# Expert slots regrouped from 28 to 24 units of 32, w1 and w3 interleaved in each weight block, and a new order table

## The chip, the cores and the metric

One core of a Trainium2 chip runs the whole program. The metric is the device time of one execution in microseconds; runs of the same kernel differ by a few tenths of a per cent. The profile is of one further execution of the same program.

## What is computed

Two blocks follow each other on 256 tokens of width 1024. The first mixes tokens with gated linear attention and then runs a mixture of experts; the second has two attention layers, for which a context of 256 tokens goes through the same layer beside the tokens. The change is in the experts of the first block:

```python
N_EXPERTS = 16; N_EXPERT_GROUPS = 4; TOP_K = 2; D_EXPERT = D_MODEL // 2      # D_MODEL = 1024

def _moe(h, w_router, b_router, w1, w3, w2):            # h: 256 tokens
    scores = jax.nn.sigmoid((h @ w_router).astype(jnp.float32))
    sel = scores + b_router.astype(jnp.float32)
    ...                                                  # the best group of 4 experts, and 2 of its 4
    gates = jnp.sum(jax.nn.one_hot(idx, N_EXPERTS, dtype=jnp.float32) * wts[..., None], axis=1)
    out = jnp.zeros_like(h)
    for e in range(N_EXPERTS):
        he = jax.nn.silu(h @ w1[e]) * (h @ w3[e])        # [256, 512]
        out = out + gates[:, e:e + 1] * (he @ w2[e])
    return out
```

Only the tokens that picked an expert need its products: 512 token and expert pairs in all. With the given inputs expert 0 has 37 tokens, and the others, sorted, have 71, 57, 50, 43, 41, 37, 32, 26, 23, 21, 21, 15, 14, 12 and 12.

## The kernel before

**Slots and ranks.** The chip counts the tokens of each expert and sorts the experts by count: rank 0 is the fullest, rank 15 is always expert 0. `RANKS` (line 23) fixes how many slots each rank has: 128 for rank 0, 64 for ranks 1 to 8 and 15, 32 for ranks 9 to 14. `SLOT0` gives where they start; 896 slots in all, 28 units of 32. Rank 8's 64 slots are cut into two halves (8 and 80) that share their weights. An expert with more tokens than slots would run through `overflow`, a loop that starts only if a count says so.

**Gather.** `gather` collects the rows of 256 slots at a time by products with one-hot matrices (`oh`) into tiles named `xg` (the first 64 slots and the last 64 into a `t` tile). There are five such groups, `ga0` to `ga4`.

**Rounds.** `plan` (line 2106) lists seven rounds, `moe0` to `moe6`. A round of kind 64 takes two experts one after the other; each is a *step*: `ffn` multiplies 64 rows with w1 and with w3, side by side in the two column halves of the array, 8 times over (the 1024 inputs in 8 parts, `kt`); then 4 transposes, the activation, and `down`, which multiplies with w2 in 4 parts, the two halves of the output side by side. A step of kind 32 does the same for two experts at once in four column quarters. `round128` takes rank 0 with all 128 columns, w1 and w3 one after the other. That is 13 steps: eight of 64 rows, one of 128, four of 32. `merge_y` ends a round: it adds 128 slots back to their tokens by one-hot products (`ps<-y,t`). All of these are fp32; a fp32 product leaves two records in the trace.

**Weights.** An expert's weights come in six blocks of 1 MB: `w1_0`, `w3_0` (kt 0 to 3), `w1_1`, `w3_1` (kt 4 to 7), `w2_0`, `w2_1`. `loadr` (line 1994) issues a block's DMA on SyncE's queue with an address from the rank; in the trace these are the rows of line 2005. Blocks of expert 0 and all other weights are issued at line 326. At most five blocks (`WC = 5`) are held at a time; a block's buffer is free when the last product with it has run.

**What sets the order.** Every instruction is recorded first and emitted later (so nearly all rows have line 326, the helper's): `Sched.emit` simulates the engines with the costs of `_cost` and lets each take the recorded instruction that is first in program order, moved by the number of its section in the table `PRI`. The context stream of block 2 (sections beginning with X: split weights `cv`, its rows `hh` and `hl`, later `KgT`, `PT` and softmax tiles `t`) is spread by `merge` between the rounds of the experts by DMA and TensorE cost. On the chip every engine runs its list strictly in that order.

```python
    plan = [([[15], [7]], 64), ([[0]], 128), ([[1], [2]], 64), ([[3], [4]], 64), ([[5], [6]], 64),
            ([[8, 80], [9, 10]], 32), ([[11, 12], [13, 14]], 32)]
```

Of the kernel before, what the change touches and what calls it, by code (L numbers as in the profile page):

```python
# [14 lines left out]
OP = mybir.AluOpType  # L15
# [4 lines left out]
CAP = 64  # L20
NE = 16
# Slots in the first round. The experts but number 0 by their number of tokens, then number 0.
RANKS = [128] + 8 * [64] + 6 * [32] + [64]
# where the slots of a rank start (rank 8: of its halves)
SLOT0 = {15: 0, 7: 64, 0: 128, 1: 256, 2: 320, 3: 384, 4: 448, 5: 512, 6: 576,
         8: 640, 80: 704, 9: 672, 10: 736, 11: 768, 12: 832, 13: 800, 14: 864}
NSLOT = 896


# ---------------------------------------------------------------- host: layout only  # L30
# [63 lines left out]
def _chunks(i):  # L94
    """The weight stream: name -> [128, n] block, each contiguous per partition."""
    out = {}
    mods = [np.asarray(i["w_mod"])[0], np.concatenate(list(np.asarray(i["mod_w_2"])), 1)]
    for b in range(2):
        m = _kt(mods[b])
        for s in range(3):  # L100
            for kt in range(8):
                if b or s:
                    out[f"mod{b}_{s}_{kt}"] = m[:, kt, s * 2048:(s + 1) * 2048]
    # the first set in two parts: the same half of its two vectors in each
    m = _kt(mods[0])[:, :, :2048].reshape(128, 8, 2, 2, 512)
    for h in range(2):
        for k2 in range(4):
            out[f"modh{h}_{k2}"] = m[:, 2 * k2:2 * k2 + 2, :, h]

    def two(name, w):  # L110
        w = _kt(w)
        out[name + "_0"] = w[:, :4]
        out[name + "_1"] = w[:, 4:]

    g = np.asarray(i["gla_w_in"])[0]
    for n, a in (("gk", 512), ("gv0", 1024), ("gv1", 1536), ("gq", 0), ("gr0", 2048), ("gr1", 2560)):
        two(n, g[:, a:a + 512])
    o = np.asarray(i["gla_w_out"])[0]
    two("go0", o[:, :512])
    two("go1", o[:, 512:])  # L120
    w1, w3, w2 = (np.asarray(i[n])[0] for n in ("w_gate_e", "w_up_e", "w_down_e"))
    for e in range(NE):
        two(f"e{e}w1", w1[e])
        two(f"e{e}w3", w3[e])
        w = _kt(w2[e])
        out[f"e{e}w2_0"] = w[:, :2]
        out[f"e{e}w2_1"] = w[:, 2:]
    a = np.asarray(i["ab_w_in_2"])[0]
    two("acq", a[:, 0:512])
    two("agq", a[:, 544:1056])  # L130
    two("akv", np.concatenate([a[:, 512:544], a[:, 1056:1312]], 1))
    two("ag0", a[:, 1312:1824])
    two("ag1", a[:, 1824:2336])
    out["auq"] = _kt(np.asarray(i["mla_w_uq_2"])[0])
    kv = np.asarray(i["mla_w_ukv_2"])[0].reshape(256, 8, 128)
    out["aukv"] = _kt(np.concatenate([kv[:, :, :64].reshape(256, 512), kv[:, :, 64:].reshape(256, 512)], 1))
    o = np.asarray(i["ab_w_out_2"])[0]
    two("ao0", o[:, :512])
    two("ao1", o[:, 512:])
    c = np.asarray(i["cd_w_in_2"])[0]  # L140
    two("cq", c[:, 0:512])
    two("ckv", c[:, 512:768])
    for n, b in (("cgb", 768), ("cgc", 1280), ("cgh", 1792), ("cg0", 2304), ("cg1", 2816)):
        two(n, c[:, b:b + 512])
    o = np.asarray(i["cd_w_out_2"])[0]
    two("co0", o[:, :512])
    two("co1", o[:, 512:])
    return out


def host(i):
    """Lays the inputs out for the chip (copies only); returns the arrays and where the parts lie."""
    W = {}
    ch = _chunks(i)
    where, off, flat = {}, 0, []
    for n, a in ch.items():
        a = a.reshape(128, -1)
        where[n] = (off, a.shape[1])
        off += a.size
        flat.append(np.ascontiguousarray(a).reshape(-1))  # L160
    W["w"] = where
    arrays = {"w": np.concatenate(flat)}
    (W["cst"], arrays["cst"]), (W["gc"], arrays["gc"]), arrays["msk"] = _consts()
    wga = np.asarray(i["gla_w_gate_a"])[0].transpose(1, 0, 2).reshape(1024, 32)
    conv = np.asarray(i["conv_w_2"])[0]
# [12 lines left out]
    wgb = np.zeros((4, 2, 16, 2, 512), np.float32)  # L178
    for z in range(2):
        wgb[:, z, :, z, :] = gb[z][None]  # L180
    arrays["wgb"] = wgb.reshape(128, 1024)
    rows = [np.asarray(i[n]).reshape(-1) for n in (
        "gla_b_gate", "final_g", "b_router", "mla_q_gain_2", "mla_k_gain_2", "gqa_q_gain_2", "gqa_k_gain_2",
        "win_q_gain_2", "win_k_gain_2", "win_sink_2")]
    arrays["row"] = np.concatenate(rows)
    for n in ("x", "ctx", "ctx_2"):
        arrays[n] = np.ascontiguousarray(np.asarray(i[n])[0])
    return arrays, W


# ---------------------------------------------------------------- the order of the instructions
# [44 lines left out]
NB = 17  # L236
NA = 8
CTXSEQ = "CKgGqsk ba"
CDSEQ = "kqc+x gB a+G o"
GLASEQ = "N q r+M k+l1 K v+L+2 R+3 f"  # L240


class Op:
    __slots__ = ("eng", "fn", "acc", "cost", "lat", "preds", "npred", "succs", "tiles", "name", "later", "cols", "table", "grp", "tiled")


class Sched:
    """Records the program's instructions and emits them in an order found by list scheduling: every engine
    takes the first instruction of the program order whose operands are ready. Tiles of a tag are given
    their buffers in program order, so an order that fits the buffers serially always completes."""  # L250

    LAT = {"PE": 197.0, "ACT": 216.0, "DVE": 128.0, "POOL": 150.0, "SP": 950.0, "SD": 950.0, "GD": 9000.0}
    TICK = 10240.0 / 3
    GAP = (87.0, 33.0, 7.0, 33.0)
    ISSUE = {"SP": 1250.0, "SD": 1250.0, "GD": 1500.0}

    def __init__(self, nc):
        self.nc = nc
        self.main = []
        self.cur = self.main  # L260
# [90 lines left out]
    def _cost(self, eng, fn, out, a, k):  # L351
        n = self._free(out)
        if fn == "dma_start":
            return out.partition_size() * n * 4 / 360.0
        if eng == "PE":
            r32 = a[1].dtype == F32R
            if fn == "transpose":
                return 56.0 if r32 else 109.5
            cyc = 1 if r32 else 4
            m = out.partition_size()  # L360
            if m <= 64 and not r32:
                return (n * cyc / 2.4 + 77.0) / 4 if m <= 32 else (n * cyc / 2.4 + 22.0) / 2
            return max(n * cyc / 2.4, 107.0 if r32 else 210.0) + 2.5
# [20 lines left out]
    def together(self):  # L384
        """The instructions recorded inside (one engine's) are issued back to back."""
        return self._Together(self)
# [18 lines left out]
    class _Into:  # L405
# [8 lines left out]
        def __exit__(self, *a):  # L414
            self.s.cur = self.old

    def into(self, lst):
        return self._Into(self, lst)

    def merge(self, lst, i0, i1, other=1.0, later=0, dma=None):  # L420
        """Spreads the instructions of lst evenly (by tensor-engine time, and `other` for each instruction
        of another engine in main) over cur[i0:i1]; they yield to those up to `later` places further on."""
        seg = self.cur[i0:i1]

        def w(op):
            return op.cost if op.eng == "PE" else 1.0

# [18 lines left out]
    def emit(self, reorder=True, window=3000):  # L446
# [30 lines left out]
        for i, op in enumerate(ops):  # L477
            op.npred = len(op.preds)
            for j in op.preds:
                ops[j].succs.append(i)  # L480
        # tiles in order of first touch, per tag
        fifo, users = {}, {}
        for i, op in enumerate(ops):
            op.tiles = []
# [1763 lines left out]
```

## Time and profile before

| | us |
|---|---|
| median of 3 runs (lowest, highest) | 923.78 (923.73, 925.45) |
| the profiled execution, from its first to its last instruction | 926.9 |
| TensorE (PE) busy in it | 872.9 |
| VectorE (DVE), ScalarE (ACT) busy | 591.1, 418.4 |
| expert blocks that SyncE issues at line 2005: first and last | 271.0, 573.3 |

The profile gives, for each engine, the time in which it worked; a wait is given with what ended it. A line of the timeline is a run of like instructions: start, length, engine, line, operation, what it writes and reads by the program's names, the columns and the size, and the number of records. The granted clock (PEclk) is 1.00 at 2.4 GHz and 0.50 at 1.2 GHz.

### The profile page before, as it was taken

The page shows a single profiled execution, that of the slowest core. Times are in us where ns is not written, and L with a number is a line of the kernel's source. Part 1 is how long each engine was busy: PE and PEld are TensorE (multiplying, and loading weights), DVE is VectorE, ACT ScalarE, POOL GpSimd, SP SyncE. Part 2 cuts the span into 40 slices and gives each one's busy share as a digit, 9 for nine tenths or more (in the row PEclk, how much of TensorE's full clock was granted, in tenths as well). Part 3 has the DMA queues.
Part 4 walks back from the last instruction along what each step waited for, and adds up shares of the span by engine and source line. Part 5 has one row for each costly group of instructions (what it writes and reads, how often), then busy time and mean ns, then how long its engine had stood idle before and what let it go on. Part 6 is the DMA issues. An engine that isn't in the chain of part 4 may idle for free. (4 is left out here: it accounts for less than half of the span.)

```text
span 926.9 us, 15330 instructions
## 1 busy us (share of the span) xinstructions
PE 872.9 (94%) x5836; PEld 617.4 (67%) x5836; DVE 591.1 (64%) x1629; ACT 418.4 (45%) x830; POOL 0.8 (0%) x5
## 2 busy tenths in 40 slices
PE   4999999899999999999998977699999999999997
PEld 2787577567865756555544533279867788899986
DVE  2667986347983715326463532698966757988875
ACT  3456544325432314124325443355648933464691
POOL 0000000000000000000000000000000000000000
PEclk9999999898999999999999999799999999999999
DMA  9943917866627887889897999695472202556101
GB/s 380 413 182 112 420 59 268 330 246 241 235 98 284 339 349 263 319 357 352 321 384 277 349 379 421 259 362 212 182 273 91 92 1 84 209 200 235 47 1 46
DMA packets 32837, 224.17 MB, mean 242 GB/s; under 512 B 3568, under 2 KB 3824, under 8 KB 7408
## 3 DMA queue, kind: packets, MB, share of 16 engines
q1 hardware_dynamic: 32608, 222.56, 63.0%
q8 instruction: 48, 0.79, 0.3%
q0 software_dynamic: 144, 0.52, 0.2%
q14 instruction: 37, 0.30, 0.1%
HBM read 222.02 MB, written 1.05 MB: 241 GB/s over the span
## 5 line engine op out<-in xcount | busy, mean ns | idle before, releaser
L326 DVE TENSOR_TENSOR cv<-w,cv 128x1024 fp32r<-128x1024 f32 (+3 forms) x128 | 144.5, 1149 | 27.7 <-ACT cv L326 27.0
L326 ACT ACTIVATE cv<-w 128x1024 fp32r<-128x1024 f32 (+3 forms) x128 | 123.5, 996 | 55.5 <-DMA w<-in_w_dram 36.5
L326 PE MATMUL ps<-hh,cv 128*128 128x256 f32 x576 | 112.0, 289 | 0.0
L326 PE MATMUL ps<-w,xg 128*64 128x512 f32 (+2 forms) x448 | 95.5, 597 | 0.1
L326 PEld LDWEIGHTS ps<-hh,cv 128*128 128x128 f32 x576 | 91.1, 191 | 6.6 <-issue 5.2
L326 ACT ACTIVATE t<-ps 128x512 f32<-128x512 f32 (+6 forms) x80 | 37.5, 472 | 114.9 <-PE ps L326 112.0
L326 PE MATMUL ps<-w,t 128*32 128x512 f32 (+2 forms) x368 | 77.9, 614 | 7.3 <-DMA w<-in_w_dram 3.7
L326 PE MATMUL ps<-hl,cv 128*128 128x256 f32 x288 | 81.8, 288 | 0.0
L326 PE MATMUL ps<-cv,hh 128*128 128x512 f32 (+2 forms) x288 | 77.1, 351 | 2.3 <-ACT cv L326 1.3
L326 PE MATMUL ps<-c_col,t 128*128 128x128 f32 x392 | 64.2, 279 | 10.8 <-ACT t L326 9.7
L326 PE MATMUL ps<-w,cs 128*32 128x512 f32 (+1 forms) x448 | 54.3, 590 | 13.6 <-DVE s L326 9.1
L326 PEld LDWEIGHTS ps<-c_col,t 128*128 128x128 f32 x392 | 44.9, 141 | 33.2 <-ACT t L326 21.7
L326 ACT ACTIVATE t<-ps,s,f 128x512 f32<-128x512 f32 (+1 forms) x80 | 55.0, 692 | 19.6 <-DVE s L326 19.5
L326 PE MATMUL ps<-cv,mixh 128*128 128x512 f32 x192 | 60.3, 395 | 0.0
L326 PEld LDWEIGHTS ps<-cv,hh 128*128 128x128 f32 x288 | 49.9, 189 | 13.7 <-ACT cv L326 2.4
L326 DVE TENSOR_REDUCE s<-ps 128x1 f32<-128x512 f32 (+1 forms) x80 | 45.3, 580 | 19.5 <-PE ps L326 18.7
L326 PEld LDWEIGHTS ps<-w,xg 128*64 128x64 f32 (+2 forms) x448 | 27.8, 129 | 43.6 <-issue 42.0
L326 PEld LDWEIGHTS ps<-hl,cv 128*128 128x128 f32 x288 | 54.7, 191 | 1.5 <-issue 1.3
L326 PE MATMUL ps<-cv,hl 128*128 128x512 f32 (+2 forms) x144 | 49.4, 349 | 0.0
L326 ACT ACTIVATE PT<-ps 128x512 f32<-128x512 f32 (+1 forms) x80 | 39.0, 512 | 21.9 <-PE ps L326 21.5
L326 PEld LDWEIGHTS ps<-w,t 128*32 128x32 f32 (+2 forms) x368 | 21.1, 127 | 40.4 <-issue 27.1
L326 PE MATMUL ps<-cv,hlh 128*128 128x512 f32 x128 | 42.1, 400 | 0.1
(269 smaller groups left out, 1569.6 us busy)
## 6 DMA issues: line engine op xcount, KB each, us to landing
w<-in_w_dram SPq DMA_DIRECT2D x198, 1024.0 KB, 7.3
ctx<-in_ctx_dram SPq DMA_DIRECT2D x3, 1024.0 KB, 5.2
w<-in_w_dram SPq DMA_DIRECT2D x4, 576.0 KB, 8.0
x<-in_x_dram SPq DMA_DIRECT2D x2, 1024.0 KB, 10.2
w<-in_w_dram SPq DMA_DIRECT2D x4, 512.0 KB, 3.7
w<-in_w_dram SPq DMA_DIRECT2D x2, 768.0 KB, 6.4
out_dram<-x SPq DMA_DIRECT2D x2, 512.0 KB, 2.6
c_cst<-in_cst_dram SPq DMA_DIRECT2D x1, 528.0 KB, 14.6
```

Source lines behind the costliest of these rows:

```text
L326: op.fn = lambda: getattr(real, fn)(*a, **k)
```

## The change

`RANKS` becomes 96 slots for rank 0, 64 for ranks 1 to 5 and 15, 32 for ranks 6 to 14: 768 slots, 24 units. The plan has six rounds. Rank 0 (96 rows, three quarters of the array's columns) and rank 14 (32 rows, the fourth) share one step, `round4`, in products of 32 columns. That leaves eleven steps: six of 64 rows, `round4`, four of 32. `gather` has four groups. w1 and w3 of an expert are stored interleaved: block `w13_q` holds both for two parts `kt`, so an expert still has six blocks of 1 MB. The table `PRI` has new numbers for nearly all sections, and three costs that the planner uses are changed (a DMA at 380 instead of 360 bytes per ns, two costs of products); nothing else of the program moves. Comments were removed.

```diff
-RANKS = [128] + 8 * [64] + 6 * [32] + [64]
+RANKS = [96] + 5 * [64] + 9 * [32] + [64]
...
-NSLOT = 896
+NSLOT = 768
...
-        two(f"e{e}w1", w1[e])
-        two(f"e{e}w3", w3[e])
+        w = np.stack([_kt(w1[e]), _kt(w3[e])], 2)
+        for q in range(4):
+            out[f"e{e}w13_{q}"] = w[:, 2 * q:2 * q + 2]
...
+PRI = {
+    '': -1355, ('', 0): -400, ('', 2): 35, ('DB', 0): -400, ('DB', 3): -1630, ('DBc', 0): 1610, ('DG', 0): -210,
...
-            return out.partition_size() * n * 4 / 360.0
+            return out.partition_size() * n * 4 / 380.0
...
-            return max(n * cyc / 2.4, 107.0 if r32 else 210.0) + 2.5
+            return max(n / 2.4 + 13.3, 111.0) if r32 else max(n * cyc / 2.4 + 5.0, 223.0)
...
-        g = b8([8, 256], n="xg") if hi - lo == 256 else t2([8, hi - lo])
+        g = b8([8, hi - lo], n="xg") if hi - lo > 64 else t2([8, hi - lo])
...
+    def w13(w, kt, i):
+        o = (kt % 2) * 1024 + i * 512
+        return w[:, o:o + 512]
...
         def prods(kt):
-            if kt % 4 == 0:
-                st[:] = loads(ranks, f"w1_{kt // 4}", f"w3_{kt // 4}")
-            k = slice((kt % 4) * 512, (kt % 4) * 512 + 512)
-            return [(x_of(r, kt, m), w[:, k]) for r, ws in zip(ranks, st) for w in ws]
+            if kt % 2 == 0:
+                st[:] = loads(ranks, f"w13_{kt // 2}")
+            return [(x_of(r, kt, m), w13(w, kt, i)) for r, (w,) in zip(ranks, st) for i in range(2)]
...
-    def round128(r):
-        gathered([r])
+    def round4(r, r2):
+
+        gathered([r, r2])
         ps = [psum(), psum()]
-        pr = prods_of([r], 128)
+        q, o = group(r)
         for kt in range(8):
-            for p, (x, w) in zip(ps, pr(kt)):
-                mm(p, x, w, kt == 0, kt == 7)
+            if kt % 2 == 0:
+                ws = loads([r, r2], f"w13_{kt // 2}")
+            for i, p in enumerate(ps):
+                with sch.together():
+                    for b in range(4):
+                        mm(p[32 * b:32 * b + 32, :], xg[q][:, kt, o + 32 * b:o + 32 * b + 32], w13(ws[b // 3][0], kt, i), kt == 0, kt == 7)
...
-    plan = [([[15], [7]], 64), ([[0]], 128), ([[1], [2]], 64), ([[3], [4]], 64), ([[5], [6]], 64),
-            ([[8, 80], [9, 10]], 32), ([[11, 12], [13, 14]], 32)]
+    plan = [([[15], [5]], 64), ([[0, 14]], 128), ([[1], [2]], 64), ([[3], [4]], 64),
+            ([[6, 7], [8, 9]], 32), ([[10, 11], [12, 13]], 32)]
```

TensorE's list at the second step of the first 32-row round (before: ranks 9 and 10; now: ranks 8 and 9). `xg` is the gathered rows, `w_...` a weight block; the rows between are the context's attention. Before:

```order
L326 MATMUL ps_663<-w_667,xg_621 32x512
L326 MATMUL ps_663<-w_668,xg_621 32x512
L326 MATMUL ps_663<-w_669,xg_621 32x512
L326 MATMUL ps_663<-w_670,xg_621 32x512
L326 MATMUL ps_1093<-PT_1094,f_807 64x256 x4
L326 MATMUL ps_663<-w_667,xg_621 32x512
L326 MATMUL ps_663<-w_668,xg_621 32x512
L326 MATMUL ps_663<-w_669,xg_621 32x512
L326 MATMUL ps_663<-w_670,xg_621 32x512
L326 MATMUL ps_1118<-c_col_66,t_1117 128x128 x2
```

and now, in the same place:

```order
L384 MATMUL ps_1065<-PT_1066,f_779 64x256 x2
L384 MATMUL ps_1099<-c_col_66,t_1096 128x128 x2
L384 MATMUL ps_640<-w_648,xg_552 32x512 x2
L384 MATMUL ps_640<-w_649,xg_613 32x512 x2
L384 MATMUL ps_640<-w_648,xg_552 32x512 x2
L384 MATMUL ps_640<-w_649,xg_613 32x512 x2
L384 MATMUL ps_1109<-c_col_66,t_1106 128x128 x2
L384 MATMUL ps_640<-w_650,xg_552 32x512 x2
L384 MATMUL ps_640<-w_651,xg_613 32x512 x2
L384 MATMUL ps_640<-w_650,xg_552 32x512 x2
L384 MATMUL ps_640<-w_651,xg_613 32x512 x2
```

Four blocks were read by turns over four parts `kt`; now two blocks serve two parts and are done, and work of the context stands between the pairs of blocks.

TensorE's list in rank 0's step (`ps_506` and `ps_507` are the sums for w1 and w3). Before:

```order
L326 MATMUL ps_506<-w_508,xg_480 128x512
L326 MATMUL ps_839<-f_70,t_838 128x128 x3
L326 MATMUL ps_507<-w_509,xg_480 128x512
L326 MATMUL ps_506<-w_508,xg_480 128x512
L326 MATMUL ps_507<-w_509,xg_480 128x512
L326 MATMUL ps_506<-w_510,xg_480 128x512
L326 MATMUL ps_507<-w_511,xg_480 128x512
```

and now:

```order
L384 MATMUL ps_507<-w_508,xg_480 32x512 x3
L384 MATMUL ps_507<-w_509,xg_480 32x512
L384 MATMUL ps_507<-w_510,xg_480 32x512 x3
L384 MATMUL ps_507<-w_511,xg_480 32x512
L384 MATMUL ps_506<-w_510,xg_480 32x512 x3
L384 MATMUL ps_506<-w_511,xg_480 32x512
L384 MATMUL ps_507<-w_510,xg_480 32x512 x3
L384 MATMUL ps_507<-w_511,xg_480 32x512
```

One product of 128 columns became four of 32 columns, three with rank 0's block and one with rank 14's.

## Rows read from the trace of the kernel before

**Rows 1.** The page's head: span, and busy time of each engine.

```profile
span 926.9 us, 15330 instructions
PE 872.9 (94%) x5836; PEld 617.4 (67%) x5836; DVE 591.1 (64%) x1629; ACT 418.4 (45%) x830; POOL 0.8 (0%) x5
```

**Rows 2.** Windows by stage, columns in the first row, of all engines.

```profile
core 0: us, PE busy (x) PEld busy (x) DVE busy (x) ACT busy (x) POOL busy (x), PEclk, DMA share, GB/s
0.00:226.00 226.00, 208.03 (x1642) 147.26 (x1643) 143.93 (x327) 101.86 (x158) 0.85 (x5) 0.97 0.69 266
226.00:271.00 45.00, 44.91 (x250) 36.69 (x248) 38.29 (x109) 20.01 (x41) 0.00 (x0) 1.00 0.42 154
271.00:448.00 177.00, 174.52 (x929) 101.08 (x930) 79.83 (x211) 47.85 (x91) 0.00 (x0) 1.00 0.85 327
448.00:573.00 125.00, 108.51 (x748) 54.16 (x748) 58.91 (x201) 49.67 (x138) 0.00 (x0) 0.99 0.90 348
573.00:605.00 32.00, 22.80 (x124) 10.46 (x123) 20.95 (x49) 13.76 (x31) 0.00 (x0) 0.84 0.76 296
605.00:927.00 322.00, 314.16 (x2153) 267.77 (x2151) 249.20 (x734) 185.29 (x372) 0.00 (x0) 1.00 0.40 144
```

**Rows 3.** The same windows view, the stage of the dynamic blocks as one.

```profile
271.00:573.00 302.00, 283.03 (x1675) 155.23 (x1676) 138.75 (x412) 97.52 (x229) 0.00 (x0) 0.99 0.87 336
```

**Rows 4.** Timeline of SyncE's queue: start, length, blocks issued; 271 and 448 on.

```profile
271.02 3.61 SPq L2005 DMA_DIRECT2D w<-in_w_dram  x4
...
447.61 125.65 SPq L2005 DMA_DIRECT2D w<-in_w_dram  x42
```

**Rows 5.** Waits of SyncE's queue, 226 to 605: us in total, times, longest.

```profile
SPq L2005 <- PE ps L326: 207.3, 63, 11.7
```

**Rows 6.** Windows of 25 us in the stage of the experts, columns as in Rows 2.

```profile
400.00:425.00 25.00, 23.27 (x115) 11.78 (x113) 9.23 (x24) 5.65 (x9) 0.00 (x0) 1.00 0.90 355
425.00:450.00 25.00, 25.00 (x140) 13.92 (x136) 13.03 (x34) 9.63 (x18) 0.00 (x0) 1.00 0.94 370
...
550.00:575.00 25.00, 18.85 (x121) 7.03 (x122) 3.78 (x14) 6.98 (x23) 0.00 (x0) 1.00 1.01 423
```

**Rows 7.** Waits of TensorE's matmuls, 448 to 605: us in total, times, longest.

```profile
PE ps L326 <- ACT t L326: 9.0, 12, 1.3
PE ps L326 <- PEq L2156: 4.1, 1, 4.1
PE ps L326 <- DMA w<-in_w_dram: 3.7, 3, 1.4
PE ps L326 <- DVE t L326: 3.5, 2, 2.1
```

**Rows 8.** Timeline of TensorE: products with w1 and w3, with w2, by kind.

```profile
332.02 7.09 PE L326 MATMUL ps<-w,xg 128*64 128x512 f32 x32
...
438.43 3.65 PE L326 MATMUL ps<-w,t 128*64 128x512 f32 x16
...
341.80 4.46 PE L326 MATMUL ps<-w,t 128*128 128x512 f32 x10
...
501.54 3.64 PE L326 MATMUL ps<-w,xg 128*32 128x512 f32 x32
```

**Rows 9.** Timeline of TensorE: merge, transposes with what follows, and a gather's products.

```profile
465.16 1.62 PE L326 MATMUL ps<-y,t 128*128 128x512 f32 x6
...
285.83 0.77 PE L326 MATMUL ps<-c_col,t 128*128 128x128 f32 x5
286.53 7.09 PE L326 MATMUL ps<-w,xg 128*64 128x512 f32 x32
...
435.28 0.35 PE L326 MATMUL ps<-oh,xh 128*128 128x256 f32 x1
...
438.22 0.28 PE L326 MATMUL ps<-oh,xlo 128*128 128x256 f32 x1
```

**Rows 10.** The page's DMA issues: median us from issue to landing.

```profile
w<-in_w_dram SPq DMA_DIRECT2D x198, 1024.0 KB, 7.3
```

More of the change, by code (lines that the diff above doesn't have):

```diff
@@ L21 @@
 NE = 16
-RANKS = [128] + 8 * [64] + 6 * [32] + [64]
-SLOT0 = {15: 0, 7: 64, 0: 128, 1: 256, 2: 320, 3: 384, 4: 448, 5: 512, 6: 576,
-         8: 640, 80: 704, 9: 672, 10: 736, 11: 768, 12: 832, 13: 800, 14: 864}
-NSLOT = 896
+RANKS = [96] + 5 * [64] + 9 * [32] + [64]
+SLOT0 = {15: 0, 5: 64, 0: 128, 14: 224, 1: 256, 2: 320, 3: 384, 4: 448,
+         6: 512, 7: 576, 8: 544, 9: 608, 10: 640, 11: 704, 12: 672, 13: 736}
+NSLOT = 768
 def _cols(v):
@@ L210 @@
+PRI = {
[52 rows of a table added]
+    'Xbw': 1225, 'Xg': 200, 'Xgc': -970, 'Xk': -105, 'Xkc': -600, 'Xq': 650, 'Xqc': -895, 'Xs': 3675, 'Xsc': 425,
[3 rows of a table added]
+}
 TAIL = 1.0
@@ L1888, in onehots @@
         if q == 0:
-            onehot(7, 1, 64)
-            onehot(0, 1, 128)
+            onehot(5, 1, 64)
+            onehot(0, 1, 96, 128)
+            onehot(14, 1, 32)
         elif q == 1:
@@ L1893, in onehots @@
         elif q == 2:
-            onehot(5, 2, 64)
-            onehot(8, 1, 32)
-            at = SLOT0[80]
-            for t in range(2):
-                V.tensor_tensor(oh[:, t, at:at + 32], iota[:, 32:64], posr[:, t, 8:9].to_broadcast([128, 32]), op=OP.is_equal)
-            onehot(9, 2, 32, 64)
-        else:
-            onehot(11, 2, 32, 64)
-            onehot(13, 2, 32, 64)
+            onehot(6, 2, 32, 64)
+            onehot(8, 2, 32, 64)
+        else:
+            onehot(10, 2, 32, 64)
+            onehot(12, 2, 32, 64)
     for q in range(4):
@@ L1930, in gates_of @@
         for i, r in enumerate(ranks):
-            row = m * (2 * i + 1) if m < 128 else 0
+            row = m * (2 * i + 1) if m < 96 else 0
+            if r == 14:
+                m, row = 32, 96
             o = gps[row:row + m, 0:1]
             for t in range(2):
-                gt = gate[:, t, 0:1] if r == 15 else gater[:, t, r % 72:r % 72 + 1]
+                gt = gate[:, t, 0:1] if r == 15 else gater[:, t, r:r + 1]
                 mm(o, oh[:, t, SLOT0[r]:SLOT0[r] + m].bitcast(F32), gt, t == 0, t == 1)
@@ L1998, in loadr @@
         off, ln = W["w"]["e0" + n]
-        step = W["w"]["e1w1_0"][0] - W["w"]["e0w1_0"][0]
+        step = W["w"]["e1w13_0"][0] - W["w"]["e0w13_0"][0]
         t = tl("w", [ln], F32, "w")
@@ L2005, in f @@
             nc.sync.dma_start(t, D["w"][bass.ds(reg[r] * step + off, 128 * ln)].rearrange("(p n) -> p n", p=128))
-        sch.special(f, [eid], [t], 2912.0, "SP")
+        sch.special(f, [eid], [t], 2759.0, "SP")
         return t
     def loads(ranks, *names):
-        ts = {r: [loadr(r, n) for n in names] for r in dict.fromkeys(x % 72 for x in ranks)}
-        return [ts[r % 72] for r in ranks]
+        return [[loadr(r, n) for n in names] for r in ranks]
     def prods_of(ranks, m):
@@ L2057, in merge_y @@
                 scatter(oT[:, half if m else 0, t * 128:(t + 1) * 128], yh[:, half], yl[:, half], t, half, psum())
-    def round128(r):
-        gathered([r])
+    def round4(r, r2):
+        gathered([r, r2])
         ps = [psum(), psum()]
-        pr = prods_of([r], 128)
+        q, o = group(r)
         for kt in range(8):
-            for p, (x, w) in zip(ps, pr(kt)):
-                mm(p, x, w, kt == 0, kt == 7)
+            if kt % 2 == 0:
[4 more added lines that the diff above has]
+                        mm(p[32 * b:32 * b + 32, :], xg[q][:, kt, o + 32 * b:o + 32 * b + 32], w13(ws[b // 3][0], kt, i), kt == 0, kt == 7)
         pt = []
-        gcol = gates_of([r], r, 128)
+        gcol = gates_of([r, r2], r, 96)
         for i, p in enumerate(ps):
@@ L2078, in round128 @@
             if f % 2 == 0:
-                w2 = loadr(r, f"w2_{f // 2}")
+                w2 = [x[0] for x in loads([r, r2], f"w2_{f // 2}")]
             for half in range(2):
-                mm(yps[half], hT[:, f, :], w2col(w2, f, half), f == 0, f == 3)
+                with sch.together():
+                    for b in range(4):
+                        mm(yps[half][32 * b:32 * b + 32, :], hT[:, f, 32 * b:32 * b + 32], w2col(w2[b // 3], f, half), f == 0, f == 3)
         merge_y(yps, SLOT0[r], 0)
@@ L2121, in _build @@
         if m == 128:
-            round128(rs[0][0])
+            round4(*rs[0])
         else:
@@ L2189, in prods @@
                         def prods(kt):
-                            if kt % 4 == 0:
-                                st[:] = [wl(0, f"w1_{kt // 4}"), wl(1, f"w3_{kt // 4}")]
-                            return [(xs[:, kt, :], w[:, (kt % 4) * 512:(kt % 4) * 512 + 512]) for w in st]
+                            if kt % 2 == 0:
+                                st[:] = [wl(kt // 2 % 2, f"w13_{kt // 2}")]
+                            return [(xs[:, kt, :], w13(st[0], kt, i)) for i in range(2)]
                         ffn(prods, 1, oc, P2[0], P2[1], oy, oth[:, :, None, :], ohT[:, :, None, :], V, S, PE)
```

1 line of the change is left out of this document (removed), and 54 rows, old and new, of the table PRI.

## Prediction, made before the changed kernel was run

> **What bounds the kernel now.** The head of the page comes first: TensorE works 872.9 of 926.9 us, the other engines far less [rows 1]. Its 54 us of idle time are not spread evenly, so the windows by stage come next [rows 2]. From 0 to 271 it idles 18.1 us; from 271 to 448 it idles only 177 - 174.52 = 2.5; from 448 to 573 it idles 16.5; from 573 to 605 it idles 9.2; after 605 it idles 7.8 of 322. The change touches the stage from 271 to 573, in which SyncE issues the 90 expert blocks whose address depends on a rank [rows 4]. This stage moves 336 GB/s x 302 us = 101.4 MB [rows 3]. What ends it, the DMA or TensorE? The DMA reaches 423 GB/s where TensorE waits, and 370 in a window in which TensorE works all 25 us [rows 6], so on average it is not at its limit. The queue's own waits agree: the line that issues expert blocks spent 207.3 us waiting for TensorE to free a buffer [rows 5]. Up to 448 TensorE is the bound and the DMA waits for it. From 448 on neither is full (TensorE 87%, DMA share 0.90): TensorE waits for short chains of ScalarE and VectorE (9.0 and 3.5 us) and for blocks (3.7 us) [rows 7]. So TensorE work taken out of this stage shortens it, as long as the DMA can follow.
>
> **The change part by part.** *Two steps of 64 rows go* (13 steps become 11). One step is 7.09 us of products with w1 and w3 and 3.65 us with w2 [rows 8]; two are 2 x 10.74 = 21.5 us. *One merge goes*: 8 products at 1.62 / 6 = 0.27 us, 2.2 us. *Ten transposes go* (8 of hidden rows, 2 of one-hots): five take 286.53 - 285.83 = 0.70 us, so ten take 1.4 us [rows 9]. *One gather of 256 slots goes*: 32 products; 25 of them fill 435.28 to 438.43, where the next step begins, 0.126 us each, so 4.0 us [rows 8, 9]. Together 29.1 us, all of it in a stage where TensorE is in line.
>
> *Rank 0's products in four quarters.* Sixteen products with w1 and w3 and eight with w2 become 24 groups of four. A product of 128 columns takes 4.46 / 5 = 0.89 us (two records each), a group of four 3.64 / 4 = 0.91 [rows 8]: 24 x 0.02 = 0.5 us more. Rank 14 rides along at no cost. Net: 28.6 us less TensorE work.
>
> *VectorE and ScalarE* lose some 30 instructions of the same steps. They work 138.8 and 97.5 of 302 us [rows 3]; TensorE covers this, so it counts as nothing. If their cover went, the stages would be no longer than before, since their work only shrinks.
>
> *The blocks.* Their number and bytes stay: 90 dynamic ones, six per expert. What changes is how long one is held. Before, a 64-row step read two blocks over four parts, 3.5 us of products, and a 32-row step with two experts read four of the five buffers by turns over four parts; now one (or two) serve two parts, 1.8 us, and are freed. This acts on the 16.5 us that TensorE idles from 448 to 573 [rows 2]. No row shows finer blocks, so the gain is bounded by 0 and 16.5 us; a loss is bounded in the rivals. I take a quarter, 4.1 us, because of what the DMA then has to do. The stage would shrink by 28.6 + 4.1 = 32.7 to 269.3 us, and 101.4 MB in that is 377 GB/s, hardly more than the 370 that a row shows beside a fully working TensorE, and well under 423 [rows 6]. Half of the idle time would already ask for 382.
>
> A second way to the same number: the four 32-row steps now need 48 blocks in a row, 1.049 MB / 423 GB/s = 2.48 us each at the best rate. Five can lie ready, so 43 x 2.48 = 107 us pass from the first of these steps to the last landing [rows 6]. Their own TensorE work fits beside this: 48 groups at 0.91 us, two merges at 2.2, twenty transposes at 0.14 and a gather of 4.0 are 55 us [rows 8, 9], and what is left of the context stream fills the rest. So in the last third the DMA ends the stage, and before it TensorE does, now without [5], [6] and one gather. This leaves a few us of gain beyond the 28.6, not sixteen.
>
> *The new order outside the stage.* Sections before 271 and after 605 hold the same instructions. Idle time that an order could win is 18.1 us (9 of them the start) plus 9.2 and 7.8 [rows 2]; it could lose as much. I take 0 and keep 4 us either way for the range. The new planner costs only set the order.
>
> **Sum.** 926.9 - 32.7 = 894.2 us of span. The profiled execution is 3.1 us above the median of the runs (926.9 against 923.8), and I keep that: **891.1 us**, 3.5% less. The forecast's own range, with 0 to 10 us of idle time won and 4 us either way for the order, is 882 to 901.
>
> **The rivals.**
>
> *The DMA ends the stage at today's rate.* From 448 to 573 it moved only 348 GB/s although TensorE idled [rows 2]. If that is what the queue reaches with five buffers, the stage needs 101.4 / 0.348 = 291 us, 11 less than now, and the other 18 us of freed TensorE time turn into waits for blocks: 926.9 - 10.6 - 3.1 = 913 us. For it speaks that the freed work leaves less to cover a late block. Against it speaks that in this window, too, buffers waited for TensorE [rows 5], and the 423 GB/s behind it [rows 6]. Chance 0.15.
> The Trainium skill ("DMA: Bandwidth & Descriptors", section "Bandwidth", "Where 436 GB/s comes from") says that a load from HBM is bound by the HBM side, at about 358 GB/s per core. By that figure 101.4 MB would take an estimated 283 us, the stage would lose 19 us, and the time would be 905; the 423 GB/s of this trace [rows 6] are above it, and the page itself gives more where the other core of the pair is idle.
>
> *More than the freed work.* The finer blocks win nearly all of the 16.5 us, or the new order wins as much elsewhere: 926.9 - 28.6 - 15 - 3.1 = 880 us. In the stage alone it asks for 101.4 / 258 = 393 GB/s beside a full TensorE, which no row shows. Chance 0.12.
>
> *Slower: TensorE stalls at the block boundaries.* TensorE runs a fixed list. It begins a new block (or pair) at 11 x 6 = 66 places, against 13 x 4 = 52 before. A late block stops it even where context work further down the list is ready. Today such a stall is 1.1 to 1.4 us and happens three times after 448 [rows 7]. If the mean over 66 places exceeds 32.7 / 66 = 0.50 us, the gain is gone; with 1.4 us at half of them it costs 46 us, and the time is 937. For it: in the last third the DMA is the later one. Against it: a stall also lets buffers run full, so it can't repeat at every place while the DMA is under its limit. Chance 0.06.
>
> *The slots don't hold.* Rank 6 has exactly 32 tokens for its 32 slots. With one token more, `overflow` would run for that expert: six blocks, each some 7.3 us to land [rows 10], through two buffers, with an unhidden step of 10.7 us: some 55 us, so 946. The counts of the given inputs fit. Chance 0.01.
>
> *No change*: gain and loss cancel. Chance 0.02.
>
> **How the numbers follow.** Forecast 0.64 (882 to 901), DMA at today's rate 0.15, more 0.12, slower 0.07, no change 0.02. A measurement of this kernel can tell some 0.2% (1.8 us) from no change. Faster is 0.64 + 0.15 + 0.12 = 0.91, same 0.02, slower 0.07. The range holds 8 in 10 when it takes in the forecast, the upper half of "more" and all but the far end of the DMA case: 878 to 912.
>
> **What would show it.** TensorE's busy time should fall by some 28 us to about 844. Products `ps<-w,xg` of 128 columns should be gone, groups of four stand in their place at about 0.91 us a group. From the first to the last dynamic block it should take near 270 us instead of 302, at 370 to 385 GB/s. TensorE's idle time in the last third should be mostly waits for blocks; SyncE's waits for TensorE should be clearly under 207 us. The stretch from the merge of the last round to the end should keep its length within some 4 us. I am wrong if the stage stays near 290 us with the DMA share under 0.92 (then boundaries or buffers, not bandwidth, end it), or if the stages before 271 or after the experts move by more than 5 us, which would mean that the order, not the slots, made the time.

## The result and the profile after

The changed kernel takes 891.86 us in the median (890.18 to 893.73, four runs), the kernel before 924.62 beside it: a ratio of 0.964 (0.962 to 0.966), 32.8 us less. The forecast was 891.1 us. In the two traces the difference is larger, 926.9 - 888.4 = 38.5 us of span. In all runs the time is the span plus 1.7 to 1.9 us; the traced execution of before would thus stand at some 928.7 us, 4 us above its median, while that of after is the fastest of its four.

The head of the page of the changed kernel, and its windows by stage (columns in the first row; the cuts are those of [rows 2] moved along with the first and the last expert block, so that 448 becomes 418):

```profile
span 888.4 us, 15257 instructions
PE 844.4 (95%) x5830; PEld 598.1 (67%) x5830; DVE 578.3 (65%) x1608; ACT 416.4 (47%) x819; POOL 0.9 (0%) x5
```

```profile
core 0: us, PE busy (x) PEld busy (x) DVE busy (x) ACT busy (x) POOL busy (x), PEclk, DMA share, GB/s
0.00:226.00 226.00, 212.09 (x1687) 152.76 (x1688) 150.49 (x345) 108.69 (x171) 0.85 (x5) 1.00 0.71 275
226.00:261.00 35.00, 34.88 (x196) 28.60 (x194) 30.45 (x90) 14.15 (x32) 0.00 (x0) 1.00 0.37 138
261.00:418.00 157.00, 156.65 (x963) 87.44 (x961) 68.67 (x172) 42.24 (x78) 0.00 (x0) 1.00 0.90 351
418.00:532.00 114.00, 102.04 (x705) 51.32 (x709) 59.18 (x224) 52.19 (x139) 0.00 (x0) 0.99 0.98 394
532.00:564.00 32.00, 21.80 (x124) 8.94 (x122) 18.63 (x44) 12.21 (x28) 0.00 (x0) 0.84 0.82 317
564.00:888.00 324.00, 316.91 (x2164) 269.03 (x2164) 250.87 (x739) 186.91 (x376) 0.00 (x0) 1.00 0.40 145
```

TensorE's busy time fell from 872.9 [rows 1] to 844.4 us. The stage of the dynamic blocks fell from 302 us [rows 3] to 271 and now moves 369 GB/s:

```profile
261.00:532.00 271.00, 258.68 (x1668) 138.76 (x1670) 127.85 (x394) 94.44 (x215) 0.00 (x0) 0.99 0.93 369
500.00:525.00 25.00, 21.66 (x133) 8.51 (x134) 6.75 (x23) 8.23 (x25) 0.00 (x0) 0.93 1.01 422
```

The timeline of SyncE's queue gives its ends (start, length, blocks): the first dynamic block is issued at 261.22, the last at 532.1 (its start; the 573.3 us in the table ahead of the prediction is the end of the last issue, which starts at 572.9).

```profile
261.22 4.15 SPq L2066 DMA_DIRECT2D w<-in_w_dram  x3
...
429.13 103.28 SPq L2066 DMA_DIRECT2D w<-in_w_dram  x42
```

So the 38.5 us of the traces are 9.8 ahead of the first block (271.0 to 261.2), 31.0 in the stage (301.9 to 270.9), and 2.3 lost behind it (354.0 to 356.3). In the stage TensorE's busy time fell by 283.0 - 258.7 = 24.3 us and its idle time from 19.0 to 12.3.

Waits of TensorE from 418 to 564 (us in total, times, longest):

```profile
PE ps L384 <- ACT t L384: 4.4, 5, 1.2
PE ps L384 <- PEq L2222: 3.7, 1, 3.7
PE ps L384 <- DMA w<-in_w_dram: 3.2, 3, 1.4
PE ps L384 <- ACT y L384: 3.1, 2, 2.0
```

and the longest of SyncE's queue from 226 to 564, in the same columns:

```profile
SPq L2066 <- PE ps L384: 171.0, 64, 10.7
```

SyncE waits 171 us for buffers instead of 207 [rows 5]. TensorE still waits for a block only three times. Rank 0's products are there in groups of four (timeline: start, length, columns, records; eight records are a group), 64 records in 7.07 us, 0.88 us a group:

```profile
304.97 2.78 PE L384 MATMUL ps<-w,xg 128*32 128x512 f32 x24
...
309.61 7.07 PE L384 MATMUL ps<-w,xg 128*32 128x512 f32 x64
```

### The profile page after: what moved, and what is told of

Its sections match the earlier page's. It is cut to its first block, busy times and chain, and to the rows that moved or that the text cites. A ratio compares the mean times of both kernels' runs of the same rounds, so it can differ in the third digit from the quotient of the medians.

```text
span 888.4 us, 15257 instructions
## 1 busy us (share of the span) xinstructions
PE 844.4 (95%) x5830; PEld 598.1 (67%) x5830; DVE 578.3 (65%) x1608; ACT 416.4 (47%) x819; POOL 0.9 (0%) x5
## 5 line engine op out<-in xcount | busy, mean ns | idle before, releaser
L384 PE MATMUL ps<-hh,cv 128*128 128x256 f32 x576 | 114.4, 288 | 0.2 <-ACT cv L384 0.2
L384 PE MATMUL ps<-w,xg 128*32 128x512 f32 (+1 forms) x544 | 87.8, 605 | 3.3 <-DMA w<-in_w_dram 3.2
L384 ACT ACTIVATE t<-ps 128x512 f32<-128x512 f32 (+5 forms) x77 | 36.0, 477 | 84.1 <-PE ps L384 67.4
L384 PE MATMUL ps<-w,cs 128*32 128x512 f32 (+1 forms) x448 | 50.9, 563 | 12.8 <-DVE s L384 9.1
L384 PE MATMUL ps<-w,t 128*32 128x512 f32 (+1 forms) x320 | 54.2, 599 | 3.6 <-issue 3.0
L384 PEld LDWEIGHTS ps<-w,xg 128*32 128x32 f32 (+1 forms) x544 | 23.0, 118 | 47.1 <-issue 37.0
L384 PEld LDWEIGHTS ps<-cv,mixh 128*128 128x128 f32 x192 | 35.7, 188 | 7.3 <-issue 0.4
```

The source lines that it names most:

```text
L384: op.fn = lambda: getattr(real, fn)(*a, **k)
```

## The experiments

The theory to be tested was the prediction's own: freed TensorE work shortens the stage by its full length (28.6 us), finer blocks add a little (4.1), the order nothing. The first rival was that the DMA stops it, the second that the new order makes the time. Differences below are to the kernel before in the same comparison (medians 925.63 for the first four runs, 926.51 for the next four, 924.39 for the last four).

The intervals of the single comparisons are 2 to 5 us either way, so differences of 3 or 4 us between runs are not clear.

| run | us | against before |
|---|---|---|
| changed kernel | 891.9 | -32.8 |
| 1: before, 28.6 us of products out of four neighbouring steps | 913.8 | -11.9 |
| 2: after, 28.4 us of products added | 918.6 | -7.0 |
| 3: before, half blocks | 918.2 | -7.4 |
| 4: after, half blocks | 881.9 | -43.8 |
| 5: before, interleaved | 919.7 | -6.8 |
| 6: after, w1 and w3 in blocks of their own | 916.5 | -10.0 |
| 7: as 1, interleaved | 909.1 | -17.4 |
| 8: before, six blocks held | 937.4 | +10.9 |
| 9: before, 28.4 us out of eight steps | 908.4 | -16.0 |
| 10: as 9, interleaved | 910.7 | -13.7 |
| 11: after, 21.3 us less | 888.3 | -36.1 |
| 12: after, no table | 954.6 | +30.2 |

### Run 1: the freed work alone, in the old order

```diff
+    LIGHT = [[3], [4], [5], [6]]
...
                 with sch.together():
                     group()
+                if light and kt % 4:
+                    sch.cur[-1].fn = lambda: None
```

`light` is set in the steps of `LIGHT`. The planner still sees the products at full cost, so every other instruction keeps its place. In `down`, parts 1 and 3 go the same way.

> The kernel before, every instruction in its old place and all blocks loaded, but three quarters of the products with w1 and w3 (parts 1, 2, 3, 5, 6, 7 of 8) and half of those with w2 (parts 1 and 3 of 4) of the steps of ranks 3, 4, 5 and 6 are left out: 4 x (0.75 x 7.09 + 0.5 x 3.65) = 28.6 us of TensorE work, as much as the change takes away net, in the stretch in which TensorE is the bound. Theory (TensorE in line, its freed work is the gain): 924.6 - 28.6 = 896 us, 892 to 902. Rival (the DMA ends the stage at 348 GB/s): the stage stops at 291 us, so 914 us. Rival (the order or the finer blocks make the gain): less than 10 us, above 915 us.

913.78 us (911.05 to 916.16), ratio 0.988 (0.983 to 0.992): 11.9 us of the 28.6. It is the number of the DMA rival, and the stage has its length too (windows view):

```profile
267.00:557.00 290.00, 262.85 (x1550) 150.81 (x1548) 138.94 (x413) 97.75 (x229) 0.00 (x0) 0.97 0.89 350
```

290 us at 350 GB/s, where the rival had 291 at 348. Against [rows 3] TensorE is busy only 20.2 us less, not 28.6, at a granted clock of 0.97 instead of 0.99, and idles 27.1 us instead of 19.0. About 8 us each: part of the freed time became waits, and in another part the remaining products took longer, at the lower clock. TensorE's waits for blocks did not grow (3.6 us, before 3.7), those for ScalarE's splits did (5.4 us, before 1.3; waits view). From 375 to 475, where work was taken out, the queue moved 375 to 402 GB/s at a share of 0.94 to 0.99 (windows view), not far from its best rate (423 [rows 6]). So the theory falls for this order; whether it was the place of the four steps, the blocks or the order, the next runs ask.

### Run 2: the work put back into the changed kernel

```diff
+                    def twice(ps_=ps_, prs=prs, f=f, kt=kt):
+                        if kt < 7:
+                            f()
+                        for i, (x, w) in enumerate(prs):
+                            nc.tensor.matmul(ps_[m * i:m * i + m, :], x, w, start=False, stop=False)
+                        if kt == 7:
+                            f()
+                    op.fn = twice
```

Here, too, only what is issued changes, in the steps of ranks 1 to 4, not the place.

> The changed kernel with the products with w1 and w3 of the steps of ranks 1 to 4 each done twice (the output is another one): 4 x 7.09 = 28.4 us more TensorE work, everything else in its place. Theory (TensorE is still in line up to the last third): 891.9 + 28.4 = 920 us, 914 to 924. Rival (after the change the DMA ends the whole stage, TensorE only its own share): half or less of the added work shows, 906 us or below.

918.64 us (ten runs, 916.94 to 924.53), 0.994 (0.992 to 0.996): the added 28.4 us cost 32.8 - 7.0 = 25.8. In the new order TensorE is in line, as the theory says; taking that much out of it is worth nine tenths of its length. The list was not laid for the added work, so a part of the 25.8 may be misfit. This kernel does before's amount of TensorE work in the new order, and is only 7 us faster than before.

### Runs 3 and 4: the DMA taken out of both

```diff
-            nc.sync.dma_start(t, D["w"][bass.ds(reg[r] * step + off, 128 * ln)].rearrange("(p n) -> p n", p=128))
+            src = D["w"][bass.ds(reg[r] * step + off, 128 * ln)].rearrange("(p n) -> p n", p=128)
+            nc.sync.dma_start(t[:, :ln // 2], src[:, :ln // 2])
```

> The kernel before with only the first half of every expert block loaded by rank (0.5 MB instead of 1 MB, products read that half; the output is another one). It takes the DMA out of the stage and leaves TensorE's list as it is. Theory (up to 448 us TensorE is the bound, after that the DMA costs only part of 16.5 us): 3 to 9 us less, 916 to 921 us. Rival (the DMA ends the last third): nearly all of 16.5 us, 908 to 911 us. Rival (only chains of ScalarE and VectorE cost): less than 2 us.

> The changed kernel with only the first half of every expert block loaded by rank (products read that half; the output is another one). Theory (in the last third the DMA now ends the stage, TensorE idles 12.3 us of 270.8 in it and 10.3 in the 34 us behind it): 5 to 12 us less than 891.9, 880 to 887 us, more than in the kernel before. Rival (TensorE's own work and short chains end it, the DMA has room): under 3 us less.

918.21 us (0.992, 0.989 to 0.995) and 881.85 (0.953, 0.949 to 0.957): half the bytes win 7.4 us before and 43.8 - 32.8 = 11.0 us after. Both lie in the expected ranges: the DMA was the second limit already, and weighs more now.

### Run 5: the interleaving alone

The blocks as in the change, on the 28 units, with the old table and costs:

```diff
-            if kt % 4 == 0:
-                st[:] = loads(ranks, f"w1_{kt // 4}", f"w3_{kt // 4}")
...
+            if kt % 2 == 0:
+                st[:] = loads(ranks, f"w13_{kt // 2}")
```

> The kernel before with w1 and w3 interleaved in each block (28 units, old table, old costs): the change's second part alone. Theory as revised after the runs with products left out (924.6 to 913.8 us for 28.6 us of work) and with half blocks (918.2 us): the blocks' hold is the second limit, just behind TensorE, so lifting it alone wins at most what half blocks won, 0 to 7 us: 918 to 925 us. Rival (the interleaving makes most of the gain by itself): 15 us or more, 910 us or below. Rival (more block boundaries cost): above 927 us.

919.74 us (nine runs), 0.993 (0.992 to 0.995): 6.8 us, about what half blocks won. The time lies in the first of the three ranges. It is not the blocks alone: the planner, given other loads, laid another list with the old table (some nine tenths of TensorE's products keep their sequence). In its trace the stage is 289.8 us, 12.1 shorter than before, and the stretch behind it 359.2, 5.2 longer.

### Run 6: the new slots without the interleaving

```diff
-            if kt % 2 == 0:
-                ws = loads([r, r2], f"w13_{kt // 2}")
+            if kt % 4 == 0:
+                ws = loads([r, r2], f"w1_{kt // 4}", f"w3_{kt // 4}")
```

and `prods` as before.

> The changed kernel with w1 and w3 in blocks of their own as before (24 units, new table and costs): the change's first part without the second. Revised theory: without finer blocks the freed TensorE work is worth about what the run with products left out showed, 12 us, and the stage stays near 289 us: 908 to 916 us. The prediction's own split (28.6 us for the freed work, 4.1 us for the blocks): 896 us, 893 to 899.

916.48 us, spread from 911.4 to 922.7 at mean granted clocks of 0.985 to 0.975. It is 24.6 us slower than the changed kernel and just above the revised range. The prediction's own split (896) is off, but the run says less than it was meant to: the table was made for the interleaved program, and the planner, given other loads, lays another list (again some nine tenths of TensorE's products keep their sequence). It doesn't tell the blocks from a table that doesn't fit.

### Run 7: freed work and finer blocks together, in the old order

The edits of runs 1 and 5 together, in the list of run 5; parts 0 and 6 are kept instead of 0 and 4:

```diff
+                if light and kt % 6:
+                    def few(prs=list(pr)):
+                        for i, (x, w) in enumerate(prs):
+                            nc.tensor.matmul(ps[m * i:m * i + m, :32], x, w[:, :32], start=False, stop=False)
+                    sch.cur[-1].fn = few if kt in (2, 4) else lambda: None
```

> The kernel before with interleaved blocks and with the same 28.6 us of products left out as in the first run (parts 0 and 6 of 8 with w1 and w3 are kept, parts 2 and 4 keep 32 of 512 columns so that every block is read; old table). Revised theory (freed work and finer blocks need each other): together 24 to 32 us, 893 to 901 us. Rival (the two add up: 913.8 less what interleaving alone wins): 907 to 914 us.

909.14 us (903.97 to 914.74): 10.6 less than run 5, 4.6 less than run 1. The two roughly add up (11.9 + 6.8 = 18.7 expected for a sum, 17.4 measured). The revised theory, that freed work only lacks finer blocks, falls. It leaves 15 us to the changed kernel unexplained.

### Run 8: six blocks held

```diff
-WC = 5
+WC = 6
```

> The kernel before with six weight blocks held at a time instead of five (WC = 6), nothing else. Revised theory (how long a block's buffer is held limits the queue): a sixth buffer wins what half blocks won or less, 2 to 7 us: 917 to 922 us. Rival (the hold doesn't matter, only TensorE's list): within 2 us of 924.6.

937.41 us, 1.012 (1.007 to 1.016): slower, which neither expected. SyncE waits 218.7 us for TensorE, no less than before. With another limit the planner lays another list here, too, so this is no test of the buffers. What a sixth buffer is worth stays open.

### Runs 9 and 10: is it the place?

```diff
+                if light and kt % 2:
+                    sch.cur[-1].fn = lambda: None
```

`light` is now set in all eight steps of 64 rows.

> The kernel before with the products of parts 1, 3, 5 and 7 of 8 with w1 and w3 left out in all eight steps of 64 rows: 8 x 3.55 = 28.4 us, as much as in the first run, but spread over eight steps instead of four neighbouring ones; everything else, all loads too, in its place. Theory P (the place decides: in the first run the freed work lay in a stretch of 100 us where the DMA share then stood at 0.94 to 0.99): 22 to 28 us less than the kernel before, 898 to 904 us. Rival C (a ceiling: with blocks held this long the queue moves no more than some 350 GB/s in the stage, wherever the work is taken from): 911 to 916 us, as the first run.

> The same spread 28.4 us left out, with w1 and w3 interleaved in each block. Theory P: 22 to 28 us less than interleaving alone (919.7), 892 to 898 us, about the changed kernel's 891.9. Rival C' (freed work beside finer blocks is worth no more than the 10.6 us that the run with four neighbouring steps showed, wherever it lies; the rest of the gain is the new order): 906 to 911 us.

908.37 us (0.982, 0.978 to 0.985), between the two; and 910.73 (0.985, 0.982 to 0.988), where the rival had it. Spreading the freed work won 4.1 us more than run 1 without interleaving and 3.7 less than run 7 with it; neither is clear of the intervals. Run 10 is 6.9 us below run 5, of 28.4. So neither spreading the work nor finer blocks brings its length back. Two windows show the loss, from the first of seven of the eight steps to the first step of 32 rows, in run 10 and in run 5 (columns as above):

```profile
278.84:449.16 170.32, 157.18 (x824) 98.83 (x823) 83.63 (x197) 51.70 (x92) 0.00 (x0) 0.97 0.89 345
283.80:461.33 177.53, 175.51 (x936) 106.39 (x935) 83.59 (x197) 51.63 (x92) 0.00 (x0) 1.00 0.86 328
```

Of 7 x 3.55 = 24.9 us taken out, 7.2 are won: TensorE idles 13.1 us instead of 2.0, at a clock of 0.97 instead of 1.00. Of its waits 6.9 us are put down to ScalarE's splits and activations and 1.9 to blocks (waits view). One of these steps shows how it comes about. TensorE's timeline there (start, length, idle time before in brackets):

```profile
347.52 3.65 PE L327 MATMUL ps<-w,xg 128*64 128x512 f32 x16
...
353.51 0.28 PE L327 MATMUL ps<-hl,cv 128*128 128x256 f32 x1
356.89 0.66 PE L327 MATMUL ps<-c_col,t 128*128 128x128 f32 x4 [3.10 <-ACT t L327]
...
359.67 0.63 PE L327 MATMUL ps<-hh,cv 128*128 128x256 f32 x2
```

and ScalarE's:

```profile
354.26 2.00 ACT L327 ACTIVATE cv<-w 128x1024 fp32r<-128x1024 f32 x2 [6.87 <-DMA w<-in_w_dram]
356.17 0.67 ACT L327 ACTIVATE t<-ps,f 128x512 f32<-128x512 f32 x1
```

The block that the split waits for was issued by SyncE at 346.79, and landed at 354.15:

```profile
346.79 0.34 SPq L327 DMA_DIRECT2D w<-in_w_dram  x1
```

The same place in run 5, where the step still has all its products, on TensorE and on ScalarE:

```profile
357.36 7.09 PE L327 MATMUL ps<-w,xg 128*64 128x512 f32 x32
...
367.02 0.66 PE L327 MATMUL ps<-c_col,t 128*128 128x128 f32 x4
```

```profile
364.38 2.01 ACT L327 ACTIVATE cv<-w 128x1024 fp32r<-128x1024 f32 x2 [7.15 <-DMA w<-in_w_dram]
366.30 0.67 ACT L327 ACTIVATE t<-ps,f 128x512 f32<-128x512 f32 x1
```

On ScalarE's list two splits of a context block stand ahead of the step's activation `t<-ps,f`. With 7.09 us of products the block (issued at 356.62, landed at 364.28) is there by the time the step ends, and TensorE doesn't wait. With 3.65 us the block is late for TensorE; the split holds up the activation, and TensorE waits 3.10 us. The 3.44 us taken out are gone within the step: from its first product to the transposes 367.02 - 357.36 = 9.7 us pass in run 5, 356.89 - 347.52 = 9.4 in run 10. And behind the wait a pair of context products takes 0.63 us instead of 0.40: it runs at half clock. The profile puts the wait down to ScalarE, but what was late is a transfer. The other steps were not followed in this detail.

The Trainium skill ("PSUM — Partial Sum Buffer", section "Engine vs sequencer instructions") says that ScalarE's queue is strictly first in, first out; these rows agree, since the activation began at 356.17, right behind the splits, while the products that it reads had ended at 351.17.

### Run 11: still less work in the changed kernel

The edit of run 9 in the changed kernel, in its six steps of 64 rows:

```diff
+                if light and kt % 2:
+                    sch.cur[-1].fn = lambda: None
```

> The changed kernel with the products of parts 1, 3, 5 and 7 with w1 and w3 left out in its six steps of 64 rows: 6 x 3.55 = 21.3 us less TensorE work. If TensorE is still in line: 871 us, 869 to 876. If the DMA now sets the stage (DMA share 0.93 already, half blocks won 10 us): less than half of it, 881 us or above.

888.30 us, 0.961 (0.958 to 0.964): 3.3 us less than the changed kernel, of 21.3 freed, as the second reading has it. The new order stands at the kink: more work costs nine tenths of its length, less work wins a sixth. Its stage (windows view) moves 376 GB/s, and TensorE's clock falls to 0.96:

```profile
261.00:526.00 265.00, 247.15 (x1572) 136.54 (x1574) 128.11 (x395) 95.01 (x217) 0.00 (x0) 0.96 0.94 376
```

### Run 12: without the table

```diff
-PRI = {
-    '': -1355, ('', 0): -400, ('', 2): 35, ('DB', 0): -400, ('DB', 3): -1630, ('DBc', 0): 1610, ('DG', 0): -210,
...
+PRI = {}
```

> The changed kernel with an empty table PRI: the same instructions in the order that the planner finds unaided. If slots and blocks carry the gain and the table only adjusts: 897 to 910 us. If the fitted order carries it: back at the time of the kernel before or above, 920 us or more.

954.56 us, 1.032 (1.029 to 1.035): 63.0 us slower than with the table, and slower than before. Having a fitted order is worth more than the whole change, and not only in the stage: the first block goes out at 287.69 instead of 261.22. It says what an order without the table costs, not how the new table compares with the old: the kernel before wasn't run without its own.

## Why the prediction came out right, step by step

The changed kernel and four runs, all with interleaved blocks, give the account:

| | order laid for the full work | order laid for the freed work |
|---|---|---|
| full TensorE work | -6.8 (run 5) | -7.0 (run 2) |
| 28.4 to 28.6 us freed | -13.7 (run 10), -17.4 (run 7) | -32.8 (changed kernel) |

**TensorE work removed: right with a condition that the prediction didn't state.** Busy time fell by 28.5 us, forecast 28.6. It is worth 25.8 us (run 2) in an order laid for it, and 7 to 16 us in the old one (runs 1, 7, 9, 10). The prediction argued that TensorE is the bound up to 448 and the DMA can follow. On average it can (369 GB/s); block by block, in lists that each engine follows strictly, it could not in the old order: at the place shown in run 10, splits and activations stand where the old speed of TensorE put them. The changed kernel's order is laid anew for less work, and there the term holds. Its queue is loaded more evenly, too: in windows of 25 us from 300 to 500 the DMA share lies between 0.88 and 0.99, in run 10 between 0.71 and 0.98. That it is the order is an inference: the programs of the lower row also differ in how many steps, merges and gathers they have, and no run moved the new order alone onto the old program. Nor does the old table fit the interleaved blocks of the left column; but in the list of the kernel before itself the freed work was worth 11.9 and 16.0 us (runs 1 and 9), far from its length too.

**The finer blocks: mis-sized, as far as run 5 shows.** Forecast 4.1 us, without the new slots they win 6.8 (run 5). With the 25.8 this makes 32.6 of the 32.8 us; the two terms were off by 2.8 and 2.7 us, in opposite directions. The sum joins runs of different lists. What the blocks are worth inside the changed kernel is not shown: run 6 lost 24.6 us without them, in a list that changed as well.

**The order outside the stage: half right.** The forecast was 0, within 4 us; the stretch ahead of the stage became 9.8 us shorter in the traces, beyond the 5 us that were to mean "wrong". TensorE's idle time there fell from 18.1 [rows 2] to 14.0 us; these 4.1 us are put down to the order. The rest is the clock of one execution. Two windows of before (PEclk is the third column from the right):

```profile
165.00:180.00 15.00, 12.29 (x206) 5.93 (x193) 3.65 (x12) 3.51 (x9) 0.65 (x1) 0.77 0.95 379
215.00:228.00 13.00, 11.34 (x62) 9.89 (x61) 9.57 (x39) 5.61 (x15) 0.00 (x0) 0.74 0.50 168
```

and the same two of run 3, whose list is the same up to there:

```profile
165.00:180.00 15.00, 12.69 (x218) 6.83 (x207) 3.76 (x13) 5.05 (x11) 0.65 (x1) 1.00 0.96 394
215.00:228.00 13.00, 11.57 (x61) 9.42 (x62) 11.98 (x39) 7.89 (x17) 0.00 (x0) 1.00 0.61 230
```

The traced execution of before ran two stretches at half clock that run 3 ran at full clock, and in run 3 the first block went out at 265.24 instead of 271.02. Against that one the change wins 4.0 us ahead of the stage: up to the first block TensorE works 247.2 us in both and idles 18.1 in run 3, 14.0 now. Behind it the forecast of no more than 4 us either way held (2.3).

**From the trace to the median.** The prediction took 3.1 us off the span. That already holds the 1.8 us between span and time, so it took the trace of before to be 4 to 5 us above its median, and it is 4.1 above the median measured beside the changed kernel. The trace of after is 1.7 us below its own. These 5.8 us are what the traces show beyond the forecast (38.5 for 32.7). With run 3 as the measure ahead of the stage, the change won 4.0 us there for 0, 31.0 in the stage for 32.7, and lost 2.3 behind it for 0; these misses cancel, as do those of the two terms above, and that the median came within 1 us is partly luck. The range was added up slightly wrong: its own terms give 881 to 899 us, not 882 to 901; the result lies in both.

**What was to be seen.** Stage 270.9 us (forecast 270), 369 GB/s (370 to 385, so just under), SyncE's waits 171 us (clearly under 207), groups of four at 0.88 (0.91): as forecast. Not as forecast: TensorE's idle time in the last third is not put down to blocks (3.2 us) but to ScalarE (4.4 and 3.1); run 10 shows that such a wait can be a late block all the same. That the DMA ends the last third, the second way, agrees with the share of 0.98 from 418 to 532, with 11.0 us for half blocks, and with run 11. But the 107 us which this way counted from the first of the 32-row steps to the last landing were 115 (427.1 to 541.8), so the best rate did not hold throughout.

**The rivals.** "The DMA ends the stage at today's rate" (913 us) is what the freed work alone gave in run 1 (913.8), at 350 GB/s. Its price was right there; its mechanism, waits for expert blocks with five buffers, is not shown, since in run 1 TensorE's waits for blocks stayed at 3.6 us and those for ScalarE grew, and the spread work of run 9 came out at 908.4. The changed kernel escaped it with 369 GB/s from the same five buffers. "TensorE stalls at the boundaries" needed 0.50 us at 66 places; TensorE waited for a block three times after 418, 1.4 us at most, and run 5 with more boundaries, if in another list, was faster than before. More than the freed work and the overflow didn't occur.

The Trainium skill ("Perfetto Trace Analysis", section "Optimization Strategy") says that where the contended engine changes over time, interleaving such regimes may help beside work within each. Which engine is contended did change here, at 448 us in the kernel before; but no run changed the interleaving alone, so the 15 to 19 us between the two columns of the lower row do not test this.

## What to carry to other kernels

Work taken off the bounding engine is worth its length only where the next limit is further away than that, and in a hand-laid order the next limit is local: ask of each step which transfer stands ahead of it on the helpers' lists, and whether it will be there earlier. After such an edit it is safer to lay the order anew before the edit is judged; here the same freed work was worth 7 to 16 us in the old order and 26 in the new. An edit that makes the planner lay another list, as in runs 5, 6 and 8, tests two things at once. To learn whether an engine is at its kink, add work and remove work: 28.4 us more cost 25.8, 21.3 us less won 3.3.

## What was not expected of the hardware

**Executions of one kernel differ by the granted clock, and idle time costs twice.** The four executions of run 7 took 903.97, 907.33, 910.95 and 914.74 us at mean granted clocks of 0.987, 0.982, 0.981 and 0.976. A fall by 0.011 of 909 us is an estimated 10 us, and 10.8 were measured. Runs with freed work in the old order sit at 0.974 to 0.990 (runs 1, 7, 9, 10), before at 0.982 to 0.992, the changed kernel at 0.986 to 0.991. Idle time and half clock come together in run 10 beside run 5 (13.1 us idle at 0.97, 2.0 at 1.00). In the trace of after the clock falls at a short wait for a block, and over the 3.24 us of the products behind it 0.57 was granted (windows view):

```profile
517.00 3.24 PE L384 MATMUL ps<-w,xg 128*32 128x512 f32 x12 [1.35 <-DMA w<-in_w_dram]
```

But two executions of one list can differ at nearly the same busy time: in the two windows of before and run 3 above, TensorE was busy 12.29 and 12.69, 11.34 and 11.57 us, and the clock was 0.77 and 1.00, 0.74 and 1.00. What decided between them no run here shows.

The Trainium skill ("TensorE: Matmul & The Clock Gate", section "HAM oscillation — how this bites in real kernels") tells of a kernel whose products start at half clock behind each wait for a transfer. The rows at 517 and at 356.89 show half clock behind waits of 1.35 and 3.10 us; that every wait brings it does not hold here: behind one of 1.25 us for a block, at 468.94 in the trace of after, the clock stayed at 1.00 (timeline and windows view):

```profile
468.94 1.91 PE L384 MATMUL ps<-w,xg 128*32 128x512 f32 x12 [1.25 <-DMA w<-in_w_dram]
```

```profile
468.94:470.85 1.91, 1.91 (x12) 0.39 (x12) 0.00 (x0) 0.00 (x0) 0.00 (x0) 1.00 1.00 407
```
